# A decoder trunk on one core: the tiles that matmuls read move to addresses that are multiples of 512 bytes

## The chip, the core and the metric

The kernel runs on 1 core of one Trainium2 chip. The metric is device time in microseconds of one execution, lower is better. Three runs of the kernel before gave 1241.96, 1243.86 and 1244.34 us; the median, 1243.86 us, is the time that counts.

## What is computed

One sequence of 256 tokens of width 2048 goes through two layers in float32: a gated MLP with spatial mixing (width 4096, 8 groups, chunks of 128 tokens), and stick-breaking attention (16 heads of 128). Each ends in a residual sum and a layer norm.

```
h = x @ w_in + b_in;  u, v, g = split(h, 3)              # w_in: 2048 x 12288
u = gelu(u);  v = layer_norm(gelu(v))
mixed = per group of 512 columns: tril(w_s[group]) @ v + b_s
x = layer_norm(ALPHA * x + (u * mixed * silu(g)) @ w_out) # w_out: 4096 x 2048
k, v = split(x @ kv_w, 2);  q, g = split(x @ b_w_in, 2)   # each 2048 x 4096
A[t,s] = sigmoid(z_ts) * prod_{s<j<t} (1 - sigmoid(z_tj)),  z = q.k / sqrt(128)
x = layer_norm(ALPHA * x + ((A @ v) * silu(g)) @ b_w_out) # b_w_out: 2048 x 2048
```

## The kernel before

Every float32 product is made of three matmuls: each operand is split into a high part, rounded to float32r, and the rest, and `mm3` (L85 to L89) adds high x high (L86), high x low (L87) and low x high (L88) in PSUM. A row of the profile such as `acc<-wh,xTh` names the output, then the operand that streams through the array (moving), then the operand that is loaded into it beforehand (stationary).

Weights come in chunks of 2 x 128 rows by 512 columns. `load_chunk` (L109) brings one by DMA from the SP queue into a `raw` tile (4 buffers), and `split` (L75) makes `wh` with a cast on ScalarE (L76) and `wl` with a subtraction on VectorE (L77), five buffers of each. `gemm` (L131) then issues 12 matmuls of 512 columns per chunk: 2 rows of blocks x 2 blocks of 128 tokens x 3. There the weights move and the activations are stationary: `xTh` and `xTl` (the transposed input of the layer, 16 blocks of 128 x 256) for v, u and g of the first layer and for v of the second, `zh`/`zl` for `w_out`, `z2h`/`z2l` for `bw_out`. `gemm_T` (L456) makes k, q and the gate of the second layer transposed: there the weights are stationary, in pieces of 128 columns, and `xTh`/`xTl` move, 256 columns at a time. The matmuls of the spatial mixing (`mix`), of the attention scores (`zp`), of the running sums (`ntri` and `nones` stationary, L500 and L503) and of the weighted values (`op`) go through the same engine, and so do the transposes by `ident` (L332, L406).

The stages follow each other in the order v (8 groups), u and g (8 groups, with mixing and transposes), `w_out`, then four times v, k, q, attention and gate, then `bw_out`. The order of issue is a planner's, with some pins by hand (`order`, L79).

What the change touches is where tiles lie. Pools are laid out in the order in which they are opened (L45 to L50), and inside a pool that is never reused (`const`) the tiles follow in the order in which they are made, each rounded up to 32 bytes. The first free byte of a partition is 16512, and 16512 leaves 128 when it is divided by 512. From the shapes in the code this gives:

- `const`: `ident` (512 bytes) at 16512; `eps_t` (4 bytes, rounded to 32) at 17024; `xTh` (16384 bytes) at 17056 and `xTl` at 33440, both 160 beyond a multiple of 512, which is 32 beyond a multiple of 64; then `vstats` and other small tiles; `ntri` and `nones` at 50496 and 51008, 320 beyond a multiple of 512.
- `wraw` follows at 51520, and its tiles and those of `wspl`, `big` and `bcp` are 4096 or 3072 bytes long, so that each of them lies 320 beyond a multiple of 512, which is a multiple of 64 and not of 128. `raw`, `wh` and `wl`, `zh` and `zl`, `z2h` and `z2l`, and all the operands of mixing and attention are among these.
- `small` comes last, with `tri_f` in it.

Below, the remainder by 512 is called a tile's residue. A block of 128 columns of float32r is 512 bytes, and the blocks of a tile follow each other without gaps, so every block has the residue of its tile.

Of the kernel before, what the change touches and what calls it, by code (L numbers as in the profile page):

```python
# [9 lines left out]
F32 = mybir.dt.float32  # L10
F32R = mybir.dt.float32r
# [4 lines left out]
P = 128  # L16
D = 2048
S = 256
# [4 lines left out]
KD = D // P  # L23
# [18 lines left out]
def trunk_kernel(ctx, tc, x, xT, w_in, b_in, vln_g, vln_b, w_sT, b_sT, w_out, kv_w, bw_in, bw_out, ln_g, ln_b, ln_gT, ln_bT, out):  # L42
    nc = tc.nc

    const = ctx.enter_context(tc.tile_pool(name="const", bufs=1))  # L45
    wraw = ctx.enter_context(tc.tile_pool(name="wraw", bufs=4))
    wspl = ctx.enter_context(tc.tile_pool(name="wspl", bufs=WB))
    big = ctx.enter_context(tc.tile_pool(name="big", bufs=26))
    bcp = ctx.enter_context(tc.tile_pool(name="bcp", bufs=3))
    small = ctx.enter_context(tc.tile_pool(name="small", bufs=4))  # L50
    ps_acc = ctx.enter_context(tc.tile_pool(name="ps_acc", bufs=4, space=PSUM))
    ps_aux = ctx.enter_context(tc.tile_pool(name="ps_aux", bufs=4, space=PSUM))
# [7 lines left out]
    def big_tile(shape, dt, s):  # L60
        return big.tile(shape, dt, tag="big", name=nm(s))
# [26 lines left out]
        nc.tensor.matmul(acc, lhsT=al, rhs=bh, start=False, stop=stop, **kw)  # L88
        return first  # L89

    ident = const.tile([P, P], F32, name="ident")
    make_identity(nc, ident)
    zrow = big_tile([P, 512], F32, "zrow")
    nc.vector.memset(zrow, 0.0)
# [7 lines left out]
    warm = aux("warm")  # L102
    for i in range(WARM):
        nc.tensor.matmul(warm[:, 0:512], lhsT=wz[:, 0:P], rhs=wz, start=(i == 0), stop=(i == WARM - 1))

    xTh = const.tile([P, KD, S], F32R, name="xTh")
    xTl = const.tile([P, KD, S], F32R, name="xTl")

    def load_chunk(wv, c, col0, spill=False, ahead=None):  # L109
        r = wraw.tile([P, CK, NT], F32, tag="raw", name=nm("raw"))  # L110
# [103 lines left out]
        nc.vector.scalar_tensor_tensor(out=dst, in0=src, scalar=mv[:, 0:1], in1=g, op0=ALU.subtract, op1=ALU.mult)  # L214
        nc.vector.scalar_tensor_tensor(out=dst, in0=dst, scalar=rstd, in1=b, op0=ALU.mult, op1=ALU.add)

    # x^T, split
    xTv = xT.rearrange("(k p) t -> p k t", p=P)

    def load_xT(a, b, q):  # L220
# [13 lines left out]
        else:  # L234
            load_xT(c * CK, (c + 1) * CK, nc.sync)

# [1 line left out]
    vt = []  # L238
    vstats = const.tile([P, NTOK, G, 6], F32, name="vstats")
    for n in range(G):  # L240
        v = big_tile([P, NTOK, NT], F32, "v")
# [15 lines left out]

        gemm(w_in, AW + n * NT, KD, xstat, evac_v, ahead=ahead, halves=n == 0)

    # spatial weights  # L260
    wsh = big_tile([P, G, P], F32R, "wsh")
    wsl = big_tile([P, G, P], F32R, "wsl")
    wsr = big_tile([P, G, P], F32, "wsr")
# [14 lines left out]
        vmv.append(m2)  # L278
        vrs.append(r2)

# [1 line left out]
    zTh, zTl = [], []  # L282
    for n in range(G):
        gam = bcast(vln_g[n * NT : (n + 1) * NT])
        bet = bcast(vln_b[n * NT : (n + 1) * NT])
        v = vt[n]
# [6 lines left out]
        u = big_tile([P, NTOK, NT], F32, "u")  # L293
# [40 lines left out]
            hs = slice(2 * half, 2 * half + 2)  # L334
            split(zh[:, hs, :], zl[:, hs, :], tp.rearrange("p (k t) -> p k t", k=2))

# [1 line left out]
    def residual_gemm(w, nk, stat, rt, layer, finish, fill=None, cuts=1):  # L338
        groups = 3 + cuts
        stats = [small.tile([P, groups, 6], F32, tag=f"st{tok}{cuts}", name=nm("st"), bufs=1) for tok in range(NTOK)]  # L340
        gb = []

        for n in range(4):
            last = n == 3

            def evac(tok, acc, cs=slice(0, NT), n=n, last=last):
                r = rt[n][:, tok, cs]
                with tc.high_priority():
                    nc.vector.scalar_tensor_tensor(out=r, in0=r, scalar=ALPHA, in1=acc, op0=ALU.mult, op1=ALU.add)
                    if last and cuts > 1 and tok == 0:  # L350
                        for i in range(cuts):
                            nc.vector.bn_stats(stats[tok][:, n + i, :], rt[n][:, tok, i * NT // cuts : (i + 1) * NT // cuts])
                    else:
                        nc.vector.bn_stats(stats[tok][:, n + cs.start * cuts // NT, :], r)
                    if last and cs.stop == NT:
                        mv, rstd, ins = aggregate(stats[tok], "lrs", fill and (lambda mv: fill(tok, mv, gb)))
                        return finish(tok, mv, rstd, gb, ins)

            if last:
                for m in range(4):  # L360
                    cs = slice(m * NT, (m + 1) * NT)
                    lt = big_tile([P, 2, NT], F32, "lgb")
                    g, b = lt[:, 0, :], lt[:, 1, :]
                    nc.gpsimd.dma_start(g, ln_g[layer, cs].partition_broadcast(P))
                    nc.gpsimd.dma_start(b, ln_b[layer, cs].partition_broadcast(P))
                    gb.append((g, b))
            gemm(w, n * NT, nk, stat, evac, tail=TAIL if last else 0, cuts=cuts if last else 1)
        return gb
# [51 lines left out]

    gb0 = residual_gemm(w_out, KA, zstat, rt, 0, finish1, fill=fill1)

# [1 line left out]
    ntri = const.tile([P, P], F32R, name="ntri")  # L424
    nones = const.tile([P, P], F32R, name="nones")
    tri_f = small.tile([P, P], F32, tag="trif", name="tri_f", bufs=1)
    nc.vector.memset(tri_f, -1.0)
    nc.vector.tensor_copy(nones, tri_f)
    nc.gpsimd.affine_select(out=tri_f, in_=tri_f, pattern=[[-1, P]], base=0, channel_multiplier=1,
# [95 lines left out]
    for j in range(4):  # L525
        v = big_tile([P, NTOK, NT], F32R, "avh"), big_tile([P, NTOK, NT], F32R, "avl")
# [97 lines left out]
```

## Time and profile before

| | |
|---|---|
| median of 3 runs | 1243.86 us (1241.96 to 1244.34) |
| span of the profiled execution | 1240.0 us |
| TensorE busy (PE) | 1226.3 us, 99% |
| VectorE busy (DVE) | 715.4 us, 58% |
| ScalarE busy (ACT) | 582.3 us, 47% |
| GpSimd busy (POOL) | 51.5 us, 4% |
| HBM traffic over the span | 193 GB/s |

The span goes from the first to the last instruction of the program. The records of matmuls overlap, since the next begins to stream while the last one drains: the duration of a record is no measure of what a matmul costs the engine, the distance from its start to the next start is. In the timeline each row has the start and the duration in us.

### The profile page before, as it was taken

How to read it: one execution, taken by the hardware profiler on the slowest of the kernel's cores; microseconds unless marked ns; L12 is line 12 of the kernel's file. 1: busy time of each engine (PE TensorE's matmuls, PEld its weight loads, DVE VectorE, ACT ScalarE, POOL GpSimd, SP SyncE). 2: the span in 40 equal slices, each digit the busy share in tenths (PEclk: the TensorE clock that was granted, in tenths of full speed). 3: DMA queues.
4: the chain of work that ended last, by engine and by line, in shares of the span. 5: the costliest groups of instructions: out<-in, count | busy, mean ns of one | idle time of the engine just before them, and what ended most of it. 6: DMA issues, size and time to landing. Idle time of an engine off the chain costs nothing.

```text
span 1240.0 us, 16640 instructions
## 1 busy us (share of the span) xinstructions
PE 1226.3 (99%) x6597; PEld 1054.7 (85%) x6597; DVE 715.4 (58%) x789; ACT 582.3 (47%) x663; POOL 51.5 (4%) x94
## 2 busy tenths in 40 slices
PE   9999999999999999999999999999999999999996
PEld 6888888888888888888888888998998999999885
DVE  6655558557567567555545578455455545446566
ACT  5444445545544545444333455364365455446440
POOL 0000001000000000001000000010010001002000
PEclk9999999999999999999999999999999999999999
DMA  9776767676666676767655564555655554656661
GB/s 306 231 204 196 203 204 228 209 217 203 180 215 202 176 228 198 218 218 243 196 194 196 189 204 159 183 160 163 186 165 154 182 166 153 186 187 188 204 202 68
DMA packets 123693, 240.70 MB, mean 194 GB/s; under 512 B 8128, under 2 KB 11744, under 8 KB 123616
## 3 DMA queue, kind: packets, MB, share of 16 engines
q1 hardware_dynamic: 118848, 224.69, 57.6%
q0 software_dynamic: 4480, 14.70, 4.9%
q8 instruction: 51, 0.84, 0.3%
q10 hardware_dynamic: 288, 0.26, 0.1%
q14 instruction: 26, 0.21, 0.0%
HBM read 237.52 MB, written 2.10 MB: 193 GB/s over the span
## 4 chain that ended last, share of the span: by engine, by line
PE 98%; DVE 1%; DMA 0%; ACT 0%; SPq 0%; DVEq 0%; issue 0%
PE acc L86 31%; PE acc L88 31%; PE acc L87 31%; PE ztp L332 1%; PE zp L500 0%; DMA raw<-in_w_in 0%; PE op L88 0%; PE op L87 0%; PE op L86 0%; PE zp L87 0%; PE zp L88 0%; PE zp L86 0%; PE zp L503 0%; PE mix L86 0%; PE mix L88 0%; PE mix L87 0%
## 5 line engine op out<-in xcount | busy, mean ns | idle before, releaser
L77 DVE TENSOR_TENSOR wl<-raw,wh 128x1024 fp32r<-128x1024 f32 (+1 forms) x417 | 508.1, 1224 | 459.3 <-ACT wh L76 458.6
L76 ACT CAST wh<-raw 128x1024 fp32r<-128x1024 f32 (+1 forms) x417 | 437.0, 1050 | 577.6 <-PE acc L88 387.6
L87 PE MATMUL acc<-wl,xTh 128*128 128x512 f32 x896 | 356.0, 398 | 0.0
L86 PE MATMUL acc<-wh,xTh 128*128 128x512 f32 x896 | 355.2, 398 | 0.7 <-ACT xTh L76 0.7
L88 PE MATMUL acc<-wh,xTl 128*128 128x512 f32 x896 | 355.2, 397 | 0.0
L86 PE MATMUL acc<-xTh,wh 128*128 128x256 f32 x768 | 217.1, 283 | 0.0
L88 PE MATMUL acc<-xTh,wl 128*128 128x256 f32 x768 | 216.2, 282 | 0.0
L87 PE MATMUL acc<-xTl,wh 128*128 128x256 f32 x768 | 216.0, 281 | 0.0
L86 PEld LDWEIGHTS acc<-wh,xTh 128*128 128x128 f32 x896 | 169.0, 189 | 42.5 <-ACT xTh L76 2.2
L88 PEld LDWEIGHTS acc<-wh,xTl 128*128 128x128 f32 x896 | 169.0, 189 | 41.1 <-DVE xTl L77 0.4
L87 PEld LDWEIGHTS acc<-wl,xTh 128*128 128x128 f32 x896 | 169.1, 189 | 40.5
L87 PEld LDWEIGHTS acc<-xTl,wh 128*128 128x128 f32 x768 | 145.1, 189 | 0.2
L88 PEld LDWEIGHTS acc<-xTh,wl 128*128 128x128 f32 x768 | 144.7, 188 | 0.0
L86 PEld LDWEIGHTS acc<-xTh,wh 128*128 128x128 f32 x768 | 144.0, 188 | 0.2
L86 PE MATMUL acc<-wh,zh 128*128 128x512 f32 x256 | 99.9, 390 | 0.0
L87 PE MATMUL acc<-wl,zh 128*128 128x512 f32 x256 | 99.7, 389 | 0.0
L88 PE MATMUL acc<-wh,zl 128*128 128x512 f32 x256 | 99.6, 389 | 0.0
L88 PEld LDWEIGHTS acc<-wh,zl 128*128 128x128 f32 x256 | 48.0, 188 | 10.0
L87 PEld LDWEIGHTS acc<-wl,zh 128*128 128x128 f32 x256 | 48.1, 188 | 9.9
L86 PEld LDWEIGHTS acc<-wh,zh 128*128 128x128 f32 x256 | 48.1, 188 | 9.7
L87 PE MATMUL acc<-wl,z2h 128*128 128x512 f32 (+1 forms) x144 | 52.7, 366 | 0.0
L86 PE MATMUL acc<-wh,z2h 128*128 128x512 f32 (+1 forms) x144 | 52.6, 366 | 0.0
(134 smaller groups left out, 745.2 us busy)
## 6 DMA issues: line engine op xcount, KB each, us to landing
raw<-in_w_in SPq DMA_DIRECT2D x191, 512.0 KB, 4.5
raw<-in_w_out SPq DMA_DIRECT2D x64, 512.0 KB, 4.5
raw<-in_kv_w SPq DMA_DIRECT2D x64, 512.0 KB, 3.8
raw<-in_bw_in SPq DMA_DIRECT2D x64, 512.0 KB, 4.3
raw<-in_bw_out SPq DMA_DIRECT2D x32, 512.0 KB, 4.4
bc<-in_b_in POOLq DMA_DIRECT2D x16, 256.0 KB, 4.7
bc<-in_b_in SPq DMA_DIRECT2D x8, 256.0 KB, 4.8
bc<-in_vln_g POOLq DMA_DIRECT2D x8, 256.0 KB, 5.1
```

What stands on the lines that cost most here:

```text
L76: h = nc.scalar.copy(hi, src)
L77: return h, nc.vector.tensor_tensor(out=lo, in0=src, in1=hi.bitcast(F32), op=ALU.subtract)
L86: first = nc.tensor.matmul(acc, lhsT=ah, rhs=bh, start=start, stop=False, **kw)
L87: nc.tensor.matmul(acc, lhsT=ah, rhs=bl, start=False, stop=False, **kw)
L88: nc.tensor.matmul(acc, lhsT=al, rhs=bh, start=False, stop=stop, **kw)
L332: nc.tensor.transpose(out=tp[:, (kk * NTOK + tok) * P : (kk * NTOK + tok + 1) * P], in_=gt[:, tok, c : c + P], identity=ident)
```

## The change

A pool `lead` is opened first, in the place of `const`. It begins with a tile `pad` of 96 floats (384 bytes), which no instruction uses, then come `xTh`, `xTl`, `ident`, `ntri`, `nones` and `tri_f`. As 16512 + 384 = 16896 = 33 x 512, and all these tiles are multiples of 512 bytes long, each has residue 0; `wraw`, `wspl`, `big` and `bcp` come behind them and have residue 0 too. `const`, which keeps the small tiles (`eps_t`, `vstats`, `bs`, `gT` and the like), and `small` are opened behind them. No instruction, no buffer count and no order written by hand is changed; the removed comment lines are left out here.

```diff
-    const = ctx.enter_context(tc.tile_pool(name="const", bufs=1))
+    lead = ctx.enter_context(tc.tile_pool(name="lead", bufs=1))
     wraw = ctx.enter_context(tc.tile_pool(name="wraw", bufs=4))
     wspl = ctx.enter_context(tc.tile_pool(name="wspl", bufs=WB))
     big = ctx.enter_context(tc.tile_pool(name="big", bufs=26))
     bcp = ctx.enter_context(tc.tile_pool(name="bcp", bufs=3))
+    const = ctx.enter_context(tc.tile_pool(name="const", bufs=1))
     small = ctx.enter_context(tc.tile_pool(name="small", bufs=4))
...
-    ident = const.tile([P, P], F32, name="ident")
+    lead.tile([P, P - P // 4], F32, name="pad")
+    xTh = lead.tile([P, KD, S], F32R, name="xTh")
+    xTl = lead.tile([P, KD, S], F32R, name="xTl")
+    ident = lead.tile([P, P], F32, name="ident")
+    ntri = lead.tile([P, P], F32R, name="ntri")
+    nones = lead.tile([P, P], F32R, name="nones")
+    tri_f = lead.tile([P, P], F32, name="tri_f")
     make_identity(nc, ident)
...
-
-    xTh = const.tile([P, KD, S], F32R, name="xTh")
-    xTl = const.tile([P, KD, S], F32R, name="xTl")
...
-    ntri = const.tile([P, P], F32R, name="ntri")
-    nones = const.tile([P, P], F32R, name="nones")
-    tri_f = small.tile([P, P], F32, tag="trif", name="tri_f", bufs=1)
```

## Rows read from the trace of the kernel before

**Rows 1.** The page: busy time of each engine, and the chain that ended last

```profile
PE 1226.3 (99%) x6597; PEld 1054.7 (85%) x6597; DVE 715.4 (58%) x789; ACT 582.3 (47%) x663; POOL 51.5 (4%) x94
...
PE 98%; DVE 1%; DMA 0%; ACT 0%; SPq 0%; DVEq 0%; issue 0%
```

**Rows 2.** Waits of TensorE: line, for whom, total us, times, longest

```profile
PE warm L104 <- DVE wz L101: 2.0, 1, 2.0
PE acc L86 <- ACT xTh L76: 0.7, 1, 0.7
```

**Rows 3.** Timeline of TensorE, v of the first layer: first and last of 172 matmuls

```profile
99.73 0.40 PE L88 MATMUL acc<-wh,xTl 128*128 128x512 f32 x1
...
139.79 0.40 PE L88 MATMUL acc<-wh,xTl 128*128 128x512 f32 x1
```

**Rows 4.** Timeline of TensorE, `w_out`: first and last of 179 matmuls

```profile
599.62 0.39 PE L86 MATMUL acc<-wh,zh 128*128 128x512 f32 x1
...
639.97 0.39 PE L87 MATMUL acc<-wl,zh 128*128 128x512 f32 x1
```

**Rows 5.** Timeline of TensorE where `w_out` ends and v of the second layer begins

```profile
739.67 0.39 PE L87 MATMUL acc<-wl,zh 128*128 128x512 f32 x1
739.90 0.39 PE L88 MATMUL acc<-wh,zl 128*128 128x512 f32 x1
740.13 0.39 PE L86 MATMUL acc<-wh,zh 128*128 128x512 f32 x1
...
740.81 0.39 PE L86 MATMUL acc<-wh,xTh 128*128 128x512 f32 x1
...
743.15 0.40 PE L87 MATMUL acc<-wl,xTh 128*128 128x512 f32 x1
```

**Rows 6.** Timeline of TensorE, k of the second layer: first and last of 136 matmuls

```profile
780.75 0.28 PE L88 MATMUL acc<-xTh,wl 128*128 128x256 f32 x1
...
796.94 0.28 PE L88 MATMUL acc<-xTh,wl 128*128 128x256 f32 x1
```

**Rows 7.** Timeline of TensorE, end of `bw_out`: first and last of 45 matmuls

```profile
1219.14 0.28 PE L86 MATMUL acc<-wh,z2h 128*128 128x256 f32 x1
...
1224.42 0.28 PE L88 MATMUL acc<-wh,z2l 128*128 128x256 f32 x1
```

**Rows 8.** Groups by line and shape, TensorE: count | busy us, mean ns | idle before

```profile
L87 PE MATMUL acc<-wl,xTh 128*128 128x512 f32 x896 | 356.0, 398 | 0.0
...
L86 PE MATMUL acc<-xTh,wh 128*128 128x256 f32 x768 | 217.1, 283 | 0.0
...
L86 PE MATMUL acc<-wh,zh 128*128 128x512 f32 x256 | 99.9, 390 | 0.0
...
L86 PE MATMUL acc<-wh,z2h 128*128 128x512 f32 x112 | 43.6, 389 | 0.0
L332 PE MATMUL ztp<-ident,g 128*128 128x128 f32 x64 | 9.6, 272 | 0.0
...
L406 PE MATMUL xtp<-ident,r 128*128 128x128 f32 x32 | 4.2, 272 | 0.0
```

**Rows 9.** Stretches of v and of `w_out`: busy us (instructions) by engine, clock, DMA share

```profile
25.00:100.00 75.00, 75.00 (x322) 60.30 (x321) 43.34 (x44) 33.64 (x36) 0.00 (x0) 1.00 0.75 223
590.00:735.00 145.00, 145.00 (x642) 120.00 (x641) 76.77 (x79) 57.63 (x56) 0.00 (x0) 1.00 0.60 197
```

**Rows 10.** Groups by line and shape: the splits of a chunk on VectorE and ScalarE

```profile
L77 DVE TENSOR_TENSOR wl<-raw,wh 128x1024 fp32r<-128x1024 f32 x415 | 506.7, 1227 | 457.9 <-ACT wh L76 457.2
L76 ACT CAST wh<-raw 128x1024 fp32r<-128x1024 f32 x415 | 435.8, 1052 | 576.2 <-PE acc L88 387.6 <-PE acc L87 118.5 <-DMA raw<-in_w_in 17.1
```

**Rows 11.** Waits of the SP queue: what holds back the loads of weights

```profile
SPq L113 <- DVE wl L77: 980.7, 403, 10.6
```

## Prediction

> **What bounds the kernel now.** I read the page's busy times and its chain first: TensorE is busy 99% of the span, and 98% of the chain that ended last is TensorE's own work [rows 1]. The view of waits confirms it: TensorE waited for others 2.7 us in all, in two places at the start [rows 2]. So the time is the sum of the distances from one matmul's start to the next, and a change can matter only through that distance, unless it makes another engine late. The third view is therefore the timeline of TensorE alone, in stretches that hold one kind of matmul. In each the reader is to take last start minus first start, and divide by the number of steps, one less than the number of matmuls.
>
> - v of the first layer, `xT` stationary, 512 columns: (139.79 - 99.73) / 171 = 0.2343 us [rows 3].
> - `w_out`, `zh`/`zl` stationary, 512 columns: (639.97 - 599.62) / 178 = 0.2267 us [rows 4].
> - k, `xT` moving, weights stationary, 256 columns: (796.94 - 780.75) / 135 = 0.1199 us [rows 6].
> - the end of `bw_out`, `z2` stationary, 256 columns: (1224.42 - 1219.14) / 44 = 0.1200 us [rows 7].
>
> The first two are the same work: same shape, type and moving buffers, and a granted clock of 1.00 in both stages [rows 9]. They differ by 7.6 ns. Where `w_out` ends the pace changes with the stationary tile itself: the five steps from 739.67 to 740.81 take 1.14 us, 0.228 each, and the ten from 740.81 to 743.15, once `xT` is stationary, take 2.34 us, 0.234 each [rows 5]. Nothing else changes at that point: the weights still come through the same buffers. What sets `xT` apart is where it lies: residue 160, off the multiples of 64, against residue 320, a multiple of 64, for every other operand. That is an inference, since the trace has no addresses; its weak point is that `xT` is also the one stationary operand of that shape in the lowest part of the memory.
>
> **The change part by part.**
>
> `xT` as stationary operand moves from residue 160 to 0. This is 3 x 896 = 2688 matmuls of 512 columns (the group of L87 stands for the three lines) [rows 8]. If residue 0 costs what residue 320 costs, each saves 0.2343 - 0.2267 = 7.6 ns, and 2688 x 7.6 ns = 20.4 us. The mean durations of the records, 398 against 390 ns, show the same 8 ns [rows 8]. The bounds: nothing, if it isn't the residue, and 2688 x 21 ns = 56 us if all that a step takes beyond its columns goes. For that second bound I take the slope between `w_out` and the end of `bw_out`: (226.7 - 120.0) / 256 = 0.4168 ns per column, which is one column per cycle of 2.4 GHz, the upper of the clock's two levels; that leaves 226.7 - 512 x 0.4168 = 13.3 ns per matmul at residue 320, and 234.3 - 213.4 = 21 ns at residue 160.
>
> `xT` as moving operand, 3 x 768 = 2304 matmuls of 256 columns [rows 8], goes from 160 to 0. Here the trace has the comparison: moving at 160 takes 0.1199 us, moving at 320 takes 0.1200 us [rows 6, 7]. So the moving side doesn't care whether it starts on a multiple of 64, and I take nothing.
>
> All other operands go from residue 320 to 0: 6597 - 96 transposes - 5 warm-up matmuls - 2688 = 3808 matmuls have them as stationary side [rows 1, 8], and all 6496 have one of them on one side or both. No row has an operand at a multiple of 128, so this is bounded from both sides: 13.3 ns less each at best, 7.6 ns more each at worst (if 0 were as bad as 160). I take nothing, because the nearest comparison, 160 against 320 on the moving side, gave nothing, and because 13.3 ns on top of a stream at full clock can as well be the price of changing the stationary block, which is paid at any address; the rows can't tell.
>
> At this point the Trainium skill speaks against the change. "SBUF — State Buffer", section "Specifications (TRN2)", gives the memory lines of 16 bytes. Residues 160, 320 and 0 all begin on such a line, so by that rule no contiguous operand would gain, and the sum would be 0. The rows disagree, with 7.6 ns between residues 160 and 320 [rows 3, 4], so the measurement decides that 16 bytes isn't the whole of it. "TensorE: Matmul & The Clock Gate", section "Wait — 56ns, not 53.3ns?", gives columns / 2.4 GHz + about 2.5 ns for warm matmuls one behind the other, 215.8 ns for 512 columns. Here 226.7 ns is the best that any row shows. By the page some 11 ns of each step could go.
>
> `ident` (128 to 0), `ntri`, `nones` (320 to 0) and `tri_f`: 96 transposes [rows 8] and a few instructions, taken as nothing; even 10 ns for each transpose would be 1 us. The pad has no instruction. `const` goes behind the large pools, and no matmul reads it. Where no instruction is added, none waits longer on a queue; the buffer counts stay, so the loads are paced as before.
>
> What becomes late next? A chunk of 12 matmuls will take 12 x 0.2267 = 2.72 us in place of 2.81 us. VectorE needs 1.23 us for its split and ScalarE 1.05 us [rows 10], the loads wait for a free `raw` tile and not for the memory [rows 11], and `w_out` already runs at this very pace, with TensorE busy for all of the 145.00 us [rows 9]. So the cover holds and the gain reaches the end. Were it gone, the loss could be no more than the 20.4 us themselves.
>
> The sum: 1240.0 - 20.4 = 1219.6 us of span. The median lies 3.9 us above the profiled span, so 1219.6 + 3.9 = 1223.5 us.
>
> **The rivals.**
>
> 1. Alignment to more than 64 bytes pays as well. Then the 13.3 ns shrink for all 6496 matmuls. One more step of 7.6 ns gives 1223.5 - 49 = 1174 us; all of it, 1223.5 - 86 = 1137 us. For it: 320 is no multiple of 128, so no row excludes it, and this is where the page with its 2.5 ns would come true. Against it: moving from 160 to 320 brought nothing on the moving side, and within the stretches at 320 the pace is even: 0.2267 us, 2.4 GHz and a remainder [rows 4, 7].
>
> 2. It isn't the residue but the place (the low part of the memory, or the neighbourhood of two tiles of 16 KB). `xT` stays there, 160 bytes lower, and nothing changes: 1243.9 us. The 16-byte rule of the Trainium skill would end here too. Against it: as moving operand `xT` costs nothing extra in the same place [rows 6].
>
> 3. Residue 0 is the worse one: stationary block and moving block then begin at the same point of a 512-byte row, and if they get in each other's way the cost of `xT` today falls on all. `xT` keeps its 0.2343 us, and 3808 matmuls lose 7.6 ns: 1243.9 + 29 = 1273 us. It beats the gain from 20.4 us / 3808 = 5.4 ns per matmul on. Against it: in `w_out` both sides already have one and the same residue, 320, and that is the fast stretch [rows 4].
>
> That the change doesn't do what it says would need the pad to be dropped. All residues would then be 128, which is a multiple of 64, so the forecast would be the same.
>
> **How the numbers follow.** The forecast has 0.72, with an own range of 1217 to 1231 us (6.5 us to the fast side for a little more on the other operands, 7.5 us for a third of the gain lost). Rival 1 has 0.14, rival 2 has 0.08, rival 3 has 0.06. The predicted time is the forecast's, 1223.5 us. Its own range and rival 2 make 0.80 together, so the range reaches up to 1245 us; downwards it takes in the mild end of rival 1, 2 ns on each matmul, which is 13 us below 1223.5 us, and the 2.5 us that a measurement may be off: 1208 us. A difference of 0.2% (2.5 us) is about what a measurement of this kernel can tell from no change. Faster by more than that: 0.72 + 0.14 = 0.86; within it: 0.08; slower: 0.06.
>
> **What the profile after would show.** If the step is right, the timeline of v has 0.2267 us from start to start in place of 0.2343, and the stretch where `w_out` hands over to `xT` has no kink. `w_out` stays at 0.2267, and k at 0.1199 us. If `w_out` or k become faster too, rival 1 holds; if v keeps its 0.2343 us and nothing moves, rival 2; if `w_out` rises to 0.234 us, rival 3. New waits of TensorE on ScalarE or VectorE would show that the cover was thinner than I say.

## The result: 1223.12 us, and the profile after

The changed kernel takes 1223.12 us (median of 4 runs, 1222.04 to 1224.66), against 1242.91 us for the kernel before in its runs to that point. The ratio is 0.9841, with a 95% interval of 0.9826 to 0.9856. The forecast was 1223.5 us. The number holds; the reason given for it does not, as the experiments show.

The page of the changed kernel: span, busy time of each engine, and the chain that ended last.

```profile
span 1220.4 us, 16640 instructions
...
PE 1206.5 (99%) x6597; PEld 1053.1 (86%) x6597; DVE 714.7 (59%) x789; ACT 582.7 (48%) x663; POOL 51.5 (4%) x94
...
PE 98%; DVE 1%; DMA 1%; SPq 0%; DVEq 0%; issue 0%
```

The count of instructions is the same on every engine, and the 19.6 us that the span lost are the 19.8 us that TensorE is busy less [rows 1]. The timeline of TensorE says where: v of the first layer (first and last of 178 matmuls), the place where `w_out` hands over to `xT`, and k (first and last of 111). `mm3` stands one line further down than before, at L87 to L89.

```profile
99.70 0.39 PE L89 MATMUL acc<-wh,xTl 128*128 128x512 f32 x1
...
139.82 0.39 PE L89 MATMUL acc<-wh,xTl 128*128 128x512 f32 x1
```

```profile
721.80 0.39 PE L87 MATMUL acc<-wh,zh 128*128 128x512 f32 x1
...
723.84 0.39 PE L87 MATMUL acc<-wh,xTh 128*128 128x512 f32 x1
...
727.92 0.39 PE L87 MATMUL acc<-wh,xTh 128*128 128x512 f32 x1
```

```profile
768.77 0.28 PE L88 MATMUL acc<-xTl,wh 128*128 128x256 f32 x1
...
781.98 0.28 PE L87 MATMUL acc<-xTh,wh 128*128 128x256 f32 x1
```

v: (139.82 - 99.70) / 177 = 0.2267 us from start to start, where it was 0.2343 [rows 3]. The handover has no kink any more: nine steps of `w_out` take 2.04 us, 0.2267 each, and the next eighteen, with `xT` stationary, take 4.08 us, 0.2267 each [rows 5]. k: 13.21 / 110 = 0.1201 us, unchanged [rows 6]. Nothing new is late: TensorE's waits are still two entries at the start.

```profile
PE warm L111 <- DVE wz L108: 2.0, 1, 2.0
PE acc L87 <- ACT xTh L77: 0.9, 2, 0.7
```

Summed over the whole run, from each start to the next, the steps with `xT` stationary went from 633.0 to 613.4 us, those with `xT` moving from 276.4 to 276.3 us, and all others stay at 317.4 us. So the whole difference lies in the group that the forecast named.

### The profile page after: what moved, and what is told of

Same layout as the page of the kernel before. It is cut to its first block, busy times and chain, and to the rows that moved or that the text cites. A ratio compares the mean times of both kernels' runs of the same rounds, so it can differ in the third digit from the quotient of the medians.

```text
span 1220.4 us, 16640 instructions
## 1 busy us (share of the span) xinstructions
PE 1206.5 (99%) x6597; PEld 1053.1 (86%) x6597; DVE 714.7 (59%) x789; ACT 582.7 (48%) x663; POOL 51.5 (4%) x94
## 4 chain that ended last, share of the span: by engine, by line
PE 98%; DVE 1%; DMA 1%; SPq 0%; DVEq 0%; issue 0%
PE acc L89 31%; PE acc L88 31%; PE acc L87 31%; PE ztp L336 1%; DMA xTr<-in_xT 1%; PE zp L501 0%; PE op L88 0%; PE zp L89 0%; PE op L87 0%; PE zp L88 0%; PE op L89 0%; PE zp L87 0%; PE zp L504 0%; PE mix L87 0%; PE mix L89 0%; PE mix L88 0%
## 5 line engine op out<-in xcount | busy, mean ns | idle before, releaser
L88 PE MATMUL acc<-wl,xTh 128*128 128x512 f32 x896 | 349.7, 391 | 0.0
L87 PE MATMUL acc<-wh,xTh 128*128 128x512 f32 x896 | 348.8, 391 | 0.9 <-ACT xTh L77 0.9
L89 PE MATMUL acc<-wh,xTl 128*128 128x512 f32 x896 | 348.9, 390 | 0.1
L88 PE MATMUL acc<-xTl,wh 128*128 128x256 f32 x768 | 217.4, 283 | 0.0
L87 PE MATMUL acc<-xTh,wh 128*128 128x256 f32 x768 | 217.3, 283 | 0.0
L89 PE MATMUL acc<-xTh,wl 128*128 128x256 f32 x768 | 217.2, 283 | 0.0
L87 PEld LDWEIGHTS acc<-wh,xTh 128*128 128x128 f32 x896 | 168.4, 188 | 36.8 <-ACT xTh L77 2.3
L89 PEld LDWEIGHTS acc<-wh,xTl 128*128 128x128 f32 x896 | 168.5, 188 | 35.2 <-DVE xTl L78 0.5
L88 PEld LDWEIGHTS acc<-wl,xTh 128*128 128x128 f32 x896 | 168.5, 188 | 34.4
L87 PEld LDWEIGHTS acc<-xTh,wh 128*128 128x128 f32 x768 | 147.2, 192 | 0.2
L88 PEld LDWEIGHTS acc<-xTl,wh 128*128 128x128 f32 x768 | 147.2, 192 | 0.2
L89 PEld LDWEIGHTS acc<-xTh,wl 128*128 128x128 f32 x768 | 147.1, 192 | 0.0
L87 PE MATMUL acc<-wh,zh 128*128 128x512 f32 x256 | 99.9, 390 | 0.0
L88 PE MATMUL acc<-wl,zh 128*128 128x512 f32 x256 | 99.7, 390 | 0.0
L89 PE MATMUL acc<-wh,zl 128*128 128x512 f32 x256 | 99.6, 389 | 0.0
L88 PEld LDWEIGHTS acc<-wl,zh 128*128 128x128 f32 x256 | 48.1, 188 | 9.9
L87 PEld LDWEIGHTS acc<-wh,zh 128*128 128x128 f32 x256 | 48.1, 188 | 9.9
L89 PEld LDWEIGHTS acc<-wh,zl 128*128 128x128 f32 x256 | 48.1, 188 | 9.8
L88 PE MATMUL acc<-wl,z2h 128*128 128x512 f32 (+1 forms) x144 | 52.7, 366 | 0.0
L87 PE MATMUL acc<-wh,z2h 128*128 128x512 f32 (+1 forms) x144 | 52.7, 366 | 0.0
```

The costliest lines, as they stand in the source:

```text
L87: first = nc.tensor.matmul(acc, lhsT=ah, rhs=bh, start=start, stop=False, **kw)
L88: nc.tensor.matmul(acc, lhsT=ah, rhs=bl, start=False, stop=False, **kw)
```

## The experiments

Most of the shifts are made by small unused tiles in front of the tiles named; where only `xT` is to move, a second one behind it brings all others back to their residue. e2, e3, e5 to e9 and e12 were run once each; the runs of the kernel before lie between 1241.7 and 1245.0 us, so a few us between two of the times say little, and the argument rests on the steps. The mean granted clock is 0.996 to 0.998 in every run, so the clock makes none of the differences. The traces hold no addresses; the residues are those that the order and the sizes of the tiles in the code give. Steps are read from the timeline of TensorE as above: v between 100 and 140 us, k between 785 and 799 us, or 769 and 782 us where the kernel is faster.

**One tile in the old kernel (e1), one operand in the new one (e2, e3), the weights and most others in the new one (e4).** e1 is the forecast's theory in its smallest form: it puts `xT` on a multiple of 128 and leaves all the other operands. In e4 `ident`, `ntri` and `nones` stay at 0 with `xT`.

```diff
 # e1_eps_behind, against the kernel before
+    xTh = const.tile([P, KD, S], F32R, name="xTh")
+    xTl = const.tile([P, KD, S], F32R, name="xTl")
     eps_t = const.tile([P, 1], F32, name="eps_t")
...
-    xTh = const.tile([P, KD, S], F32R, name="xTh")
-    xTl = const.tile([P, KD, S], F32R, name="xTl")
```

> The kernel before with one tile moved: eps_t stands behind xTh and xTl, so these begin 32 bytes lower, at residue 128, and all other operands stay at residue 320. Theory (a stationary block off a multiple of 64 bytes costs 7.6 ns): v steps 0.2267 us from start to start and the time is that of the changed kernel, 1223 us. Rival (all operands have to be at multiples of 512, or the gain came from the weights' side): v stays between 0.2343 and 0.2267 us and the time lies above 1230 us. Rival (place): the tiles lie where they lay, so 1243 us.

```diff
 # e2_x32, against the changed kernel (e3_x64: 16 and 112 floats)
+    lead.tile([P, 8], F32, name="shift")
     xTh = lead.tile([P, KD, S], F32R, name="xTh")
     xTl = lead.tile([P, KD, S], F32R, name="xTl")
+    lead.tile([P, 120], F32, name="back")
```

> The changed kernel with xTh and xTl alone shifted by 32 bytes, to residue 32; all others stay at 0. Theory: v back at 0.2343 us, w_out and k unchanged at 0.2267 and 0.1199 us, time 1223 + 20 = 1243 us. Rival (place, or what lies around): 1223 us, v at 0.2267 us. Rival (residue 160 itself, as a place in a row of 512 bytes): v somewhere else than 0.2343 us.

> The changed kernel with xTh and xTl alone shifted by 64 bytes, to residue 64; all others stay at 0. Theory (multiples of 64 are enough): v at 0.2267 us, 1223 us. Rival (stationary and moving side have to have the same residue): v slower than 0.2267 us, up to 1243 us.

```diff
 # e4_weights32, against the changed kernel
+    gap = ctx.enter_context(tc.tile_pool(name="gap", bufs=1))
     wspl = ctx.enter_context(tc.tile_pool(name="wspl", bufs=WB))
...
+    gap.tile([P, 8], F32, name="shift")
```

> The changed kernel with wspl, big and bcp shifted by 32 bytes: weights, z, z2 and the operands of mixing and attention at residue 32, xTh and xTl at 0. Theory (the stationary side alone counts, at any column count): v stays at 0.2267 us although its moving side is at 32; k goes from 0.1199 to 0.1275 us, w_out from 0.2267 to 0.2343 us; (2304 + 1200 + 240) matmuls x 7.6 ns = 28 us, so 1251 us. Rival (either side off a multiple of 64 costs it): v rises to 0.2343 us too, about 1272 us. Rival (only a difference between the two sides counts): v rises to 0.2343 us, w_out stays at 0.2267 us, about 1243 to 1261 us.

Measured: e1 1233.99 us (ratio to before 0.9926, 0.9912 to 0.9941), e2 1232.96 us, e3 1233.90 us, e4 1235.90 us (0.9941, 0.9925 to 0.9958). Not one is where the theory had it. Two rivals named the pattern that the later runs bear out: that of e3 (both sides have to have the same residue), whose time holds too, and the last of e4 (v rises, `w_out` stays), whose time was too high. The first rival of e1 and the last of e2 had the numbers right, but their reasons, multiples of 512 and a place in a row of 512 bytes, fell with e5, e8 and e11. v of e1 (174 matmuls), of e2 (173), of e3 (173) and of e4 (173), and `w_out` of e4 (134), first and last each:

```profile
99.63 0.39 PE L87 MATMUL acc<-wl,xTh 128*128 128x512 f32 x1
...
140.00 0.39 PE L86 MATMUL acc<-wh,xTh 128*128 128x512 f32 x1
```

```profile
99.79 0.40 PE L87 MATMUL acc<-wh,xTh 128*128 128x512 f32 x1
...
139.92 0.40 PE L88 MATMUL acc<-wl,xTh 128*128 128x512 f32 x1
```

```profile
99.83 0.39 PE L87 MATMUL acc<-wh,xTh 128*128 128x512 f32 x1
...
139.97 0.39 PE L88 MATMUL acc<-wl,xTh 128*128 128x512 f32 x1
```

```profile
99.75 0.40 PE L88 MATMUL acc<-wh,xTh 128*128 128x512 f32 x1
...
139.88 0.40 PE L89 MATMUL acc<-wl,xTh 128*128 128x512 f32 x1
```

```profile
599.73 0.39 PE L88 MATMUL acc<-wh,zh 128*128 128x512 f32 x1
...
629.88 0.39 PE L89 MATMUL acc<-wl,zh 128*128 128x512 f32 x1
```

The four stretches of v are 40.37 / 173 = 0.2334, 40.13 / 172 = 0.2333, 40.14 / 172 = 0.2334 and 40.13 / 172 = 0.2333 us. So v is slow with `xT` at residue 128 (e1) and at 64 (e3), both multiples of 64, and it is slow with `xT` at 0 when only the weights that stream are at 32 (e4). The moving side does count. In e4 `w_out`, where both sides are at 32, keeps 0.2267 us: (629.88 - 599.73) / 133. What the fast stretches have in common is that both sides have the same residue.

The second surprise is k, which became faster than in either kernel. Of e2 (123 matmuls), of e1 (121) and of e3 (122), first and last:

```profile
784.74 0.28 PE L87 MATMUL acc<-xTh,wh 128*128 128x256 f32 x1
...
798.96 0.28 PE L89 MATMUL acc<-xTh,wl 128*128 128x256 f32 x1
```

```profile
784.82 0.28 PE L88 MATMUL acc<-xTh,wl 128*128 128x256 f32 x1
...
798.95 0.28 PE L88 MATMUL acc<-xTh,wl 128*128 128x256 f32 x1
```

```profile
784.73 0.28 PE L87 MATMUL acc<-xTh,wh 128*128 128x256 f32 x1
...
798.98 0.28 PE L88 MATMUL acc<-xTl,wh 128*128 128x256 f32 x1
```

14.22 / 122 = 0.1166, 14.13 / 120 = 0.1178 and 14.25 / 121 = 0.1178 us. In k equal residues are slower than these differences, by up to 3.4 ns. This is why e2 takes 1233 and not the 1243 us of the theory: over the whole run its steps with `xT` stationary take 631.3 us, nearly the 633.0 of before, but those with `xT` moving take 7.1 us less than in the changed kernel. e1 and e3 have the same difference between the sides, 64 by the remainder of 256 (128 - 320 = -192, and 64 - 0), at quite other residues, and they agree in both stages. That gives the theory for the next runs: the difference counts, not the residue.

**All at 32 (e5), and differences of 16, 4 and 256 bytes (e6 to e8).**

```diff
 # e5_all32, against the changed kernel
-    lead.tile([P, P - P // 4], F32, name="pad")
+    lead.tile([P, P - P // 4 + 8], F32, name="pad")
 # e6_x16 (e7_x4: 1 in place of 4)
-    xTh = lead.tile([P, KD, S], F32R, name="xTh")
+    xTh = lead.tile([P, KD * S + P], F32R, name="xTh")[:, 4 : 4 + KD * S].rearrange("p (k t) -> p k t", k=KD)
...
 # e8_x256: as e2_x32, with 64 and 64 floats
```

> The changed kernel with a pad that is 32 bytes longer: all operands at residue 32, none on a multiple of 64. Theory now (a step of 512 columns takes 0.2267 us where stationary and moving block have the same residue, and 0.2333 us or more where they differ; the residue itself doesn't matter): v and w_out at 0.2267 us, k at 0.1199 us, 1223 us as for the changed kernel. Rival (both have to lie on a multiple of 64 or more): v and w_out at 0.2333 us or more, at least 1223 + 3800 x 6.7 ns = 1248 us.

> The changed kernel with xTh and xTl alone shifted by 16 bytes inside longer tiles; all others at residue 0. Theory (any difference counts): v at 0.2333 us, k at 0.117 us, about 1233 us. Rival (a difference below 32 bytes is none): v at 0.2267 us, k at 0.1199 us, 1223 us.

> The changed kernel with xTh and xTl alone shifted by 4 bytes, one element, off the multiples of 16; all others at residue 0. Theory (any difference counts): v at 0.2333 us, about 1233 us. Rival (a difference below 16 or 32 bytes is none): v at 0.2267 us, 1223 us. Second rival (a start off a multiple of 16 has a price of its own): v above 0.2343 us, k above 0.1199 us, over 1243 us.

> The changed kernel with xTh and xTl alone shifted by 256 bytes; all others at residue 0. Theory (the whole residue by 512 has to be the same): v at 0.2333 us, k at 0.117 us, about 1233 us. Rival (the pattern repeats every 256 bytes or less): v at 0.2267 us, k at 0.1199 us, 1223 us.

Measured: e5 1222.97 us, e6 1230.57 us, e7 1244.60 us, e8 1224.93 us. v of e5 (178 matmuls) and of e8 (179), and k of e7 (115):

```profile
99.65 0.39 PE L88 MATMUL acc<-wl,xTh 128*128 128x512 f32 x1
...
139.77 0.39 PE L88 MATMUL acc<-wl,xTh 128*128 128x512 f32 x1
```

```profile
99.62 0.39 PE L88 MATMUL acc<-wl,xTh 128*128 128x512 f32 x1
...
139.96 0.39 PE L89 MATMUL acc<-wh,xTl 128*128 128x512 f32 x1
```

```profile
784.83 0.29 PE L89 MATMUL acc<-xTh,wl 128*128 128x256 f32 x1
...
798.89 0.29 PE L89 MATMUL acc<-xTh,wl 128*128 128x256 f32 x1
```

v takes 0.2267 us in e5 and 0.2266 us in e8. e5 has not one operand on a multiple of 64, and it is as fast as the changed kernel: the residue itself is nothing. e8 shows that a difference of 256 bytes is none, so my theory of the whole residue by 512 fell, and the remainder by 256 took its place. A difference of 16 is one (v 0.2334, k 0.1187 us), though in e6 v's pace isn't the same everywhere: between 200 and 235 us it is 35.19 / 154 = 0.2285 us, against 0.2331 us in e2 (both with a few matmuls of the mixing among them). A difference of 4 bytes is the worst in k: (798.89 - 784.83) / 114 = 0.1233 us. That and the time are as the second rival of e7 had it, but v, which it put above 0.2343 us, takes 0.2324.

**A difference of 128 (e9), and a kernel in which each stage has the difference that it likes (e10).**

```diff
 # e9_x128: as e2_x32, with 32 and 96 floats
 # e10_split_residue, against the changed kernel
-    lead.tile([P, P - P // 4], F32, name="pad")
+    lead.tile([P, P // 4], F32, name="pad")
...
-    def load_chunk(wv, c, col0, spill=False, ahead=None):
+    def load_chunk(wv, c, col0, spill=False, ahead=None, at=0):
...
-            wh = wspl.tile([P, CK, NT], F32R, tag="wh", name=nm("wh"))
-            wl = wspl.tile([P, CK, NT], F32R, tag="wl", name=nm("wl"))
+            wh, wl = (wspl.tile([P, CK * NT + 64], F32R, tag=t, name=nm(t))[:, at : at + CK * NT]
+                      .rearrange("p (j n) -> p j n", j=CK) for t in ("wh", "wl"))
...
-            wh, wl = load_chunk(wv, c, col0)
+            wh, wl = load_chunk(wv, c, col0, at=56)
```

> The changed kernel with xTh and xTl alone shifted by 128 bytes; all others at residue 0. Theory (what counts is the difference between stationary and moving block, and it repeats after 256 bytes): v at 0.233 us, k at some 0.117 us, about 1234 us, as for the shift of 64 bytes. Rival (it repeats after 128 bytes already): v at 0.2267 us, k at 0.1199 us, 1223 us as for the shift of 256.

> The changed kernel with weights at two places: the wspl tiles are 256 bytes longer, and gemm_T alone writes and reads its weights 224 bytes into them, so that the moving block lies 32 bytes beyond the stationary one by the remainder of 256; gemm keeps both sides at the same remainder (the pad is 256 bytes shorter, all else moves by multiples of 256). Theory (the difference counts, in each stage by itself): v and w_out stay at 0.2267 us, k, q and gate go from 0.1199 to 0.1168 us, 2304 x 3.1 ns = 7.1 us less than the changed kernel, 1216 us. Rival (what counts is where xT lies, not the difference): k stays at 0.1199 us, 1223 us. Rival (shifted weights cost their own price, as in the run with weights at 32): k at 0.1183 us or more, 1219 us or more.

Measured: e9 1238.92 us, with v at 0.2324 and k at 0.1187 us. A difference of 128 isn't none, so the pattern doesn't repeat every 128 bytes; it is dearer in time than 64, 1233.90 us, mainly because k slows down behind the stretch that is read: over the whole run the steps with `xT` moving take 275.1 us in e9 and 270.6 us in e3. e10 takes 1214.62 us (ratio to before 0.9771, 0.9758 to 0.9785), 8.5 us less than the changed kernel's median; the profiled spans, 1220.4 and 1213.1 us, are 7.3 us apart, and 7.1 us were expected. v of e9 (174 matmuls), then v (178) and k (114) of e10:

```profile
99.63 0.39 PE L88 MATMUL acc<-wl,xTh 128*128 128x512 f32 x1
...
139.84 0.39 PE L87 MATMUL acc<-wh,xTh 128*128 128x512 f32 x1
```

```profile
99.80 0.39 PE L88 MATMUL acc<-wl,xTh 128*128 128x512 f32 x1
...
139.92 0.39 PE L88 MATMUL acc<-wl,xTh 128*128 128x512 f32 x1
```

```profile
768.77 0.28 PE L87 MATMUL acc<-xTh,wh 128*128 128x256 f32 x1
...
781.95 0.28 PE L89 MATMUL acc<-xTh,wl 128*128 128x256 f32 x1
```

v of e9 is 40.21 / 173 = 0.2324 us. In e10 v keeps 0.2267 us and k takes 13.18 / 113 = 0.1166 us, with `xT` at one and the same place for both. The stage follows the difference that it is given.

**The kernel before, with 256 bytes of padding (e11), and only the low half of `xT` shifted (e12).**

```diff
 # e11_before_plus_256, against the kernel before
+    const.tile([P, 40], F32, name="shift")
     xTh = const.tile([P, KD, S], F32R, name="xTh")
     xTl = const.tile([P, KD, S], F32R, name="xTl")
+    const.tile([P, 24], F32, name="back")
 # e12_low_half_32, against the changed kernel
     xTh = lead.tile([P, KD, S], F32R, name="xTh")
+    lead.tile([P, 8], F32, name="shift")
     xTl = lead.tile([P, KD, S], F32R, name="xTl")
+    lead.tile([P, 120], F32, name="back")
```

> The kernel before with two unused tiles of 160 and 96 bytes around xTh and xTl: no pool is moved, no operand comes to a multiple of 512 by it, xT goes from residue 160 to 320 and all others from 320 to 64, which is the same remainder by 256. Theory (only the difference between stationary and moving block counts, by 256): v at 0.2267 us, w_out 0.2267 us, k 0.1199 us, and all of the changed kernel's gain, 1223 us. Rival (the new pool, or the multiples of 512, have a part of the gain): more than 1226 us.

> The changed kernel with xTl alone shifted by 32 bytes, xTh and all others at residue 0: in v only every third matmul (high weights by xTl) has a stationary block whose residue differs from the moving one. Theory (the matmul whose own two sides differ pays): the step that starts with L89 in v goes from 0.2267 towards 0.233 us and the others stay, a mean of 0.2289 us; k gains a third of 3 ns; 1223 + 5.9 - 2.4 = 1227 us. Rival (the step before it pays, during which the block is loaded): the same time, but the step that starts with L88 is the long one.

Measured: e11 1222.44 us (ratio 0.9831, 0.9815 to 0.9847), the changed kernel's whole gain from two unused tiles. Neither the new pool nor the multiples of 512 have a part in it.

e12 takes 1234.68 us, and I expected 1227: one odd block in three costs v as much as three. Its matmuls by line (count | busy us, mean ns), part of its timeline with two of the loads of stationary blocks (PEld), and the first and last start of L88 in v, 57 rounds of the three lines apart:

```profile
L88 PE MATMUL acc<-wl,xTh 128*128 128x512 f32 x896 | 358.8, 401 | 0.0
L87 PE MATMUL acc<-wh,xTh 128*128 128x512 f32 x896 | 353.8, 397 | 0.7 <-ACT xTh L77 0.7
L89 PE MATMUL acc<-wh,xTl 128*128 128x512 f32 x896 | 349.0, 390 | 0.0
```

```profile
100.17 0.40 PE L87 MATMUL acc<-wh,xTh 128*128 128x512 f32 x1
...
100.40 0.40 PE L88 MATMUL acc<-wl,xTh 128*128 128x512 f32 x1
100.40 0.19 PEld L89 LDWEIGHTS acc<-wh,xTl 128*128 128x128 f32 x1
100.64 0.39 PE L89 MATMUL acc<-wh,xTl 128*128 128x512 f32 x1
100.64 0.19 PEld L87 LDWEIGHTS acc<-wh,xTh 128*128 128x128 f32 x1
100.87 0.40 PE L87 MATMUL acc<-wh,xTh 128*128 128x512 f32 x1
```

```profile
99.70 0.40 PE L88 MATMUL acc<-wl,xTh 128*128 128x512 f32 x1
...
139.60 0.40 PE L88 MATMUL acc<-wl,xTh 128*128 128x512 f32 x1
```

A round takes 39.90 / 57 = 0.700 us, which is 0.2333 us for each step, as in e2. From start to start between 100 and 140 us, L88's step takes 0.239 us on average, L87's 0.232 and L89's 0.229; in the changed kernel all three take 0.226 to 0.227 us. The odd block belongs to L89, and L89's step is the one that grows least. The longest is L88's, during which L89's block is loaded; L87's, which comes right behind L89's, is longer as well. The matmul whose own two sides differ isn't the one that pays most, so that expectation was wrong. The rival named the right line, but with the wrong size and without L87. So the rule of the difference is shown for stages whose stationary blocks all have one residue; which pair of blocks makes the price, the streaming one with its own stationary block or with the next one that is loaded meanwhile, isn't settled.

The runs in one table. The difference is the residue of `xT` less that of the weights, by the remainder of 256. Each pace is that of one stretch; beside it stands the sum of all steps of that kind in the run, in us, because in e6, e9 and e12 other stretches go at another pace. All other steps together take 317.3 to 317.7 us in every run.

| difference | run | v, 512 columns | all with `xT` stationary | k, 256 columns | all with `xT` moving | time |
|---|---|---|---|---|---|---|
| 0 | after, e5, e8, e11 | 0.2266 to 0.2267 us | 613.4 to 616.3 | 0.1200 to 0.1201 us | 276.3 | 1222.4 to 1224.9 us |
| 4 | e7 | 0.2324 | 628.2 | 0.1233 | 283.8 | 1244.6 |
| 16 | e6 | 0.2334 (later 0.2285) | 626.8 | 0.1187 | 271.3 | 1230.6 |
| 32 | e2 | 0.2333 | 631.3 | 0.1166 | 269.2 | 1233.0 |
| 64 | e1, e3 | 0.2334 | 631.0, 630.8 | 0.1178 | 270.6 | 1234.0, 1233.9 |
| 96 | before | 0.2343 | 633.0 | 0.1199 | 276.4 | 1242.9 |
| 128 | e9 | 0.2324 | 631.5 | 0.1187 | 275.1 | 1238.9 |
| 224 | e4 | 0.2333 | 631.4 | 0.1183 | 272.6 | 1235.9 |
| 0 in v, 32 in k | e10 | 0.2267 | 613.8 | 0.1166 | 268.9 | 1214.6 |
| 0 for `xTh`, 32 for `xTl` | e12 | 0.2333 | 630.1 | 0.1200 | 272.3 | 1234.7 |

One rival is that other engines, which read and write the same tiles, have a part in it. In the kernel before, 27 steps with `xT` stationary fall where no instruction of VectorE, ScalarE or GpSimd runs, from 0.3 us ahead of the step to its end: they take 0.2340 us on average, and 12 such steps of the changed kernel take 0.2268 us. The transfers write `raw`, which in e4 has the residue of `xT`, 0, while weights and `z` lie at 32; there v is slow and `w_out` fast, so the distance to `raw` isn't what counts.

## Why the prediction was right, and where its steps failed

**TensorE's own pace is the bound, and a shorter step reaches the end: right.** 98% of the chain is still TensorE's, and the waits are as they were.

**The size, 7.6 ns for 2688 matmuls: right.** v, u and g went from 0.2343 to the pace of `w_out`, 0.2267 us, and the span lost 19.6 us where 20.4 were worked out. The choice to price the new state by the nearest fast row carried the number.

**"What sets `xT` apart is where it lies: residue 160, off the multiples of 64": wrong.** The residue is nothing by itself (e5), and a multiple of 64 isn't enough (e1, e3). It is the difference between the stationary and the moving block, by the remainder of 256: 96 in the kernel before, 0 in the changed one. The step failed in its reading of two rows that differed in two things at once, the residue of `xT` and its difference from the weights; only the first was considered. The number came out because the fast row that I priced with, `w_out`, has a difference of 0, and so has the changed kernel. That both rows have it was luck as far as the stated reason goes: the same reasoning applied to e1 missed by 11 us.

**"The moving side doesn't care": wrong.** The comparison behind it, 0.1199 against 0.1200 us [rows 6, 7], set a difference of 96 beside one of 0, and those two happen to cost the same at 256 columns. At 16, 32, 64, 128 or 224 k takes 0.1166 to 0.1187 us in the stretches read. One equality of two points was no ground for "doesn't care".

**Nothing for the operands at 320: right,** since they had a difference of 0 and keep it; `w_out` still steps by 0.2267 us. "No row has an operand at a multiple of 128" was a slip: `ident` lay at residue 128, and its transposes are in [rows 8]. They have 128 columns, and nothing of that shape to compare them with.

**The rivals.** The first, a finer alignment that pays, didn't happen in the changed kernel; but what it saw, time left beyond the columns, is there: e10 takes 3.4 ns of it in each matmul of k. The second, the place, fell with e11, where `xT` stays in its pool, 160 bytes further up, and v takes 0.2267 us. The third, equal residues that get in each other's way, is the reverse of what v shows; in k equal residues cost 3.4 ns more than a difference of 32, but less than one of 4. Its counter-argument, that in `w_out` both sides have one residue and are fast, held the answer and was used only to dismiss it.

**If the pad had been dropped** the forecast said the same time, for being at a multiple of 64. That was not run; e5, where all operands lie at 32, bears it out for another reason: what counts is that all move together.

## What to carry to other kernels

Where TensorE is the bound, divide a stretch of the timeline by its steps and compare stages of the same shape: a few ns per matmul are invisible in the busy share (99% before and after) and were 1.6% here. Where a tile that matmuls read lies matters only against the tile it meets, by the remainder of 256 bytes, and the best difference isn't the same in each stage: among those tried it was 0 where `xT` is stationary and 512 columns stream, and 32 where `xT` moves, 256 columns at a time, and the weights are stationary. These runs don't part the column count from the change of roles. Two rows that differ in two things don't tell which one counts, even when the sum that they give comes out right; shift one side alone before naming the cause.

## What the runs showed of the hardware

- With float32r operands, 2.4 GHz granted and a new stationary block for each matmul, the step depends on the distance between the two operands' addresses, by the remainder of 256 bytes (256 is as 0 in e8, 128 is not in e9): 0.2267 to 0.2343 us at 512 columns, 0.1166 to 0.1233 us at 256. The Trainium skill describes two independent read ports for the two sides ("TensorE: Matmul & The Clock Gate", section "Step-by-step: what each phase is for"), so that loading the next block takes nothing from the stream. The runs show a pace that depends on where both sides lie; whether it is these ports that tie them together they don't show.
- The one start off a multiple of 16 bytes, e7, gave the slowest k, 0.1233 us. The 16-byte lines of "SBUF — State Buffer" (section "Specifications (TRN2)") in the Trainium skill would let one expect a price there; the run can't part it from the price of a difference of 4.
- What stays open: why equal remainders are best in v and not in k, why one odd block in three slows all three steps, and most the one ahead of its own (e12), and why the pace drifts within one run, of v at a difference of 16 (e6) and of k at 128 (e9). The runs show which step is long, not what it waits for. Differences other than those of the table weren't tried.
